# A decoder layer on one core: the first tile's two products by k tile, bias rows in eight transfers, memory preparation between down units

## The chip, the cores and the metric

The kernel runs on one core of a Trainium2 chip. The metric is device time in microseconds of one execution, the median of several runs. All data is float32. The matrix products are made in three passes of a reduced format (`fp32r`): each operand is split into a high and a low part, and hi x hi, lo x hi and hi x lo are summed.

## What is computed

One layer of a decoder, for 512 tokens of width 1024: a gated feed-forward block (FFN1), three mixers beside each other (sparse attention, a gated short convolution, attention into 256 memory tokens), and a second feed-forward block. The parts that matter here:

```python
def rmsnorm(x, g):
    y = xf * lax.rsqrt(jnp.mean(xf * xf, axis=-1, keepdims=True) + EPS)
    return y * g
def swiglu_ffn(h, w_in, w_out):                     # 1024 -> 2 x 2816 -> 1024
    a, b = jnp.split(h @ w_in, 2, axis=-1)
    return (jax.nn.silu(a) * b) @ w_out
x = x + 0.5 * swiglu_ffn(rmsnorm(x, ffn1_norm_g), ffn1_w_in, ffn1_w_out)
...
km, vm = jnp.split(rmsnorm(mem, mem_norm_g) @ w_mem_kv, 2, axis=-1)   # 256 memory tokens
...
bias = rel_bias[rel_bucket(dist)]                   # 16 heads, by distance; used in the attention
```

## The kernel before, in words

The tokens lie along the free axis: `xT` holds x as 8 k tiles of 128 x 512. `ffn(1, ...)` walks a fixed list of steps (`ffn_steps`). It has 22 feature tiles. Tiles 0 to 3 are made plainly (`up`): two products a and b, each of 8 k tiles by three passes, 24 matmuls of 512 columns (`mm3`, L419 to L421), into PSUM buffers `psg` and `pso`. Then a = silu(a) needs the row scale R. R comes from squares of x (`square_into`, ScalarE and VectorE), a sum over partitions on TensorE (L445), a Newton step on VectorE, four transposes on TensorE (L452) and a copy on ScalarE (L453). Tiles 4 to 21 are made from 2 x 2 blocks with seven products, P1 to P7 (`prod`, L545), 12 matmuls of 256 columns each, from other forms of the input (`Input.prep`) and of the weights (sums `sumS` on VectorE, L195). Between the products stand the `down` steps: eight per group of tiles, each multiplies a group's results by one column block of the second weight and adds it to `xT` on VectorE (L590, or `x1_done`, L665, in the last group). Each `down` needs one of two PSUM buffers `pss`.

Weights are loaded by SyncE's queue (SP, L183) in units of 128 x 1024 (512 KB) into four raw buffers, and split by `Weights._make`: ScalarE casts the high part `whi` (L227), VectorE subtracts to get the low part `wlo` (L228), six buffers of each. `ahead` makes the next part up to three uses early. A raw buffer that is free lets the next load go.

Work that has to be done at some time during FFN1 is a list of closures, `extra`: `more` runs the next one or two after a step. First the forms of the input (19 entries), then the bias table (4 entries: load, a product and its evacuation, a store of 16 rows to `scr`, and one transfer that repeats every row 128 times into `scr2`, L734), and, added when the products are done, the preparation of the memory tokens (10 entries: the load of `mT`, eight parts, a row scale), which so falls into the last eight `down` steps. A part is a scaled cast on ScalarE and the low half on VectorE (`mhi`, `mlo`, L457 and L458), and a square on ScalarE that VectorE adds up (L476, L477).

A scheduler then orders the instructions of each engine by dependences and program order; every engine runs its own list strictly in that order, and the two DMA queues (SP's and ScalarE's) issue in order too. The program's order sets what the scheduler prefers. The transfers of the two queues use the same 16 DMA engines. The start is written out by hand: one weight half, x tiles 0 to 2, the second half, x tiles 3 to 7.

Of the kernel before, what the change touches and what calls it, by code (L numbers as in the profile page):

```python
# [146 lines left out]
class Weights:  # L147
# [10 lines left out]
    def add(self, ap, key, width=512):  # L158
        j, n = len(self.units), ap.shape[1]
        self.units.append(ap)  # L160
        for c0 in range(0, n, width):
            c1 = min(c0 + width, n)
            self.specs.append((key, width, "raw", (j,), slice(c0, c1), (j,) if c1 == n else ()))

    def add_fast(self, a, b, f, name):

        if name == "P1":
            self.fast = getattr(self, "fast", {})
            self.fast[f] = (len(self.units), len(self.units) + 1)
            self.units += [a, b]  # L170
        j = self.fast[f]
        free = {"P2": j[:1], "P4": j[1:]}.get(name, ())
        self.specs.append((("prod", f, name), 512, FAST[name], j, None, free))


    def _dma(self, part=None):
        j = self.i_dma
        ap = self.units[j]
        n = ap.shape[1]
        if part != 1:  # L180
            self.raw[j] = self.pool.tile([128, 1024], F32, tag="wraw", name=f"wraw{j}", bufs=RAW_BUFS)
        c = slice(0, n) if part is None else slice(512 * part, 512 * part + 512)
        self.nc.sync.dma_start(self.raw[j][:, c], ap[:, c])  # L183
        if part != 0:
            self.i_dma += 1

    def prefetch(self):
        while self.i_free in self.freed:
# [67 lines left out]
class Input:  # L256
# [68 lines left out]
    def fast_done(self):  # L325
        self.stacks["late"].close()
        self.stacks["forms"].close()


class Layer:  # L330
# [29 lines left out]
    def unit_list(self):  # L360
        i = self.ins
        add = self.ws.add

        def ffn(n):
            w, wo = i[f"wf{n}i"], i[f"wf{n}o"]
            for step in ffn_steps(n):
                if step[0] == "up":
                    for ab in range(2):
                        add(w[step[1], ab], (n, "in", step[1], ab))
                elif step[0] == "down":  # L370
                    f0, f1 = FFN_GROUPS[step[1]]
                    add(wo[step[2]][:, f0 * 128:f1 * 128], (n, "out") + step[1:])
                else:
                    self.ws.add_fast(w[step[1], 0], w[step[1], 1], *step[1:])

        ffn(1)
        for c in range(4):
            for q in range(4):
                add(i["wmkv"][c, q], ("mkv", c, q))
        def tok(n, qs):  # L380
            for q in qs:
                add(i["t" + n][q][:, :TOK[n][0] * TOK[n][1][q]], ("tok", n, q), 304 if n == "s" else 512)

        def w1(kind, qs):
            for q in qs:
                add(i["w1" + "kv"[kind]][q], ("w1", kind, q))

        tok("c", range(4))
        tok("m0", [0, 1, 2])
        w1(0, [0])  # L390
        tok("m0", [3])
        w1(0, [1])
        tok("m1", [0])
        w1(0, [2])
        tok("m1", [1])
        w1(0, [3])
        tok("m1", [2])
        w1(1, [0])
        add(i["w2k"], ("w2", 0))
        w1(1, [1])  # L400
        tok("m1", [3])
        w1(1, [2, 3])
        tok("v", [0])
        add(i["w2v"], ("w2", 1))
        tok("v", [1, 2, 3])
        for n in ("s", "w", "q0", "q1"):
            tok(n, range(len(TOK[n][1])))
        for p in range(8):
            for t in range(6):
                add(i["wfeat"][p, t], ("feat", p, t))  # L410
        for m in range(NK):
            add(i["wout"][m], ("wout", m))
        ffn(2)


# [61 lines left out]
            nc.vector.tensor_tensor(acc, acc, sq[:, :src.shape[1]], op=ALU.add)  # L477


    def ffn(self, n, pool, x, done, before, extra, fast_done):  # L480

        nc, ws = self.nc, self.ws
        groups = FFN_GROUPS
        extra = list(extra)
        g, st = {}, {}

        def more(k=1):  # L490
            for fn in extra[:k]:
                fn()
            del extra[:k]

        def half_up(f, ab):
            whi, wlo = ws.use((n, "in", f, ab))
            p = self.ps("go"[ab])
            for k in range(NK):
                if k == NK // 2:
                    ws.ahead()  # L500
                    if f:
                        more()
                c = slice(k * 128, (k + 1) * 128)
                self.mm3(p, whi[:, c], wlo[:, c], x.hi[:, k], x.lo[:, k], k == 0, k == NK - 1)
            return p

        def act_a(p):
            a = pool.tile([128, 512], F32, tag="fa", name=self.nm("fa"), bufs=2)
            th = pool.tile([128, 512], F32, tag="fth", name=self.nm("fth"), bufs=2)
            nc.vector.tensor_tensor(a, p, x.R, op=ALU.mult)  # L510
            nc.scalar.activation(th, a, AF.Tanh, scale=0.5)
            nc.vector.scalar_tensor_tensor(a, th, 1.0, a, op0=ALU.add, op1=ALU.mult)
            nc.vector.tensor_tensor(a, a, x.R, op=ALU.mult)
            return a
# [3 lines left out]
            self.split(*g[f], a)  # L518

        def up(f):  # L520
            p = half_up(f, 0)
            if f > 0:
                a = act_a(p)
            if f:
                more()
            p2 = half_up(f, 1)
            if f == 0:
                before()
                a = act_a(p)
            nc.vector.tensor_tensor(a, a, p2, op=ALU.mult)  # L530
            put(f, a)
            if f:
                more()
# [45 lines left out]
        def down(gi, m):  # L579
            f0, f1 = groups[gi]  # L580
            nf = f1 - f0
            whi, wlo = ws.use((n, "out", gi, m))
            p = self.ps("s")
            for k in range(nf):
                if k == NK // 2:
                    ws.ahead()
                c = slice(k * 128, (k + 1) * 128)
                self.mm3(p, whi[:, c], wlo[:, c], g[f0 + k][0], g[f0 + k][1], k == 0, k == nf - 1)
            if gi < len(groups) - 1:
                nc.vector.scalar_tensor_tensor(self.xT[:, m], p, 0.25, self.xT[:, m], op0=ALU.mult, op1=ALU.add)  # L590
            else:
                done(m, p)
            more(2)

        steps = ffn_steps(n)
        for step, after in zip(steps, steps[1:] + [(None,)]):
            {"up": up, "prod": prod, "down": down}[step[0]](*step[1:])
            if step[0] == "up" and after[0] != "up":
                ws.sum_pool = x.plain_done()
                ws.ahead()  # L600
            elif step == ("prod", NF - 1, "P3"):
                ws.sum_pool = None
                x.fast_done()
                extra += fast_done()
        assert not extra

    def square_into(self, k, acc, src, sq):

# [7 lines left out]
    def run(self):  # L616
# [10 lines left out]
        self.scr2 = self.dram.tile([16, 128, WL], F32, name="scr2")  # L627

        nc.scalar.dma_start(self.small, ins["small"])
        self.ws._dma(part=0)  # L630
        for k in range(NK):
            nc.sync.dma_start(self.xT[:, k], ins["xT"][:, k])
            if k == 2:
                self.ws._dma(part=1)
        self.ws.prefetch()
        nc.vector.memset(self.ones, 1.0)

# [12 lines left out]

        x = Input(self, 1, fp, C_G1)
        for k in range(NK):
            x.put(k)
            if k in (0, 3):
                self.ws._make()

        def x_rstd():
            for k in range(NK):
# [14 lines left out]
        def fast_done():  # L673
            for h in (1, 0):
                mkp[h] = self.pool(memkv[h], f"mkp{h}", "right")
            made["pp"] = self.pool(prep, "pp", "right")
            return self.mem_prep(fp, made["pp"])

        self.ffn(1, fp, x, x1_done, x_rstd, x.prep() + self.bias_table(x), fast_done)
        pp = made["pp"]  # L680
        self.dump("x1", self.xT)

# [11 lines left out]
            self.split(self.Ahi[:, k], self.Alo[:, k], t)  # L694

        kfin = self.mem_kv(mkp, pp, [mix_rstd] + [lambda k=k: mix_h(k) for k in range(NK)])
        f1.close()


# [10 lines left out]
    def bias_table(self, x):  # L710
# [22 lines left out]
            src = self.scr[h:h + 1]  # L733
            nc.scalar.dma_start(self.scr2[h:h + n], bass.AP(src.tensor, src.offset, [[WL, n], [0, 128], [1, WL]]))  # L734

        return [load, table, store] + [lambda: repeat(0, 16)]

    def load_T(self, h):
        T = self.tp.tile([128, TW], F32, tag="T", name=f"T{h}", bufs=2)
# [2 lines left out]
        return T  # L742


    def mem_prep(self, fp, pp):
        self.mhi = pp.tile([128, NK, 256], F32R, name="mhi")
        self.mlo = pp.tile([128, NK, 256], F32R, name="mlo")
        mT = pp.tile([128, NK, 256], F32, tag="mT", name="mT")
        acc = pp.tile([128, 256], F32, name="macc")
        self.mrs = pp.tile([128, 2], F32, name="mrs")  # L750

        def part(k):
            self.prep_post(fp, k, mT[:, k], C_GMEM, self.mhi, self.mlo, acc)

        load = lambda: self.tc.keep_in_program_order(self.nc.scalar.dma_start(mT, self.ins["memT"]))
        return [load] + [lambda k=k: part(k) for k in range(NK)] + [lambda: self.token_rstd(pp, acc, 2, self.mrs)]

    def mem_kv(self, pools, pp, aux):

# [709 lines left out]
    def tail(self, mx1):  # L1469
# [27 lines left out]

        def fast_done():
            yp.append(self.pool(ys, "yp", "right"))
            return []  # L1500

        def y_done(m, p):
            y = yp[0].tile([128, 512], F32, tag="y", name=self.nm("y"), bufs=2)
            nc.vector.scalar_tensor_tensor(y, p, 0.25, self.xT[:, m], op0=ALU.mult, op1=ALU.add)
            nc.sync.dma_start(self.out[m], y)

        self.ffn(2, fp, x, y_done, x.rstd, x.prep(), fast_done)
        ys.close()
        f2.close()

# [81 lines left out]
```

## Time and profile before

| | us |
|---|---|
| median of 3 runs | 1412.68 |
| lowest, highest run | 1411.17, 1413.94 |
| the profiled execution, its whole time | 1415.84 |
| its span, first to last instruction | 1413.8 |
| TensorE (PE) busy | 1400.4 |
| VectorE (DVE) busy | 1094.1 |
| ScalarE (ACT) busy | 763.4 |

The profile lists every instruction of one execution with its start and duration, and for an engine's idle time the event that ended it. PE is the matmul unit, PEld its weight loads, which overlap. Matmul ends are modelled: a 512-column matmul is shown 0.39 us long though the next starts 0.23 us later, so TensorE's busy time hides small losses, and a wait of it begins up to 0.16 us before the idle time shown. PEclk is the granted TensorE clock, 1.00 for 2.4 GHz and 0.50 for 1.2 GHz. FFN1 ends at about 358 us.

### The profile page before, as it was taken

What the parts mean: (1) busy time and instruction counts of PE and PEld (TensorE: products, weight loads), DVE (VectorE), ACT (ScalarE), POOL (GpSimd) and SP (SyncE); (2) the same over time, 40 slices, a digit from 0 to 9 for tenths busy, and PEclk for the clock granted to TensorE, in tenths of its full rate; (3) what the DMA queues carried; (4) which work ended last, traced back from release to release, by engine and by line L of the source; (5) the groups of instructions that cost most, each with busy time, mean ns of one, the idle gap of its engine ahead of it and who ended that gap; (6) DMA issues with size and microseconds to landing.
All of it is one profiled execution on the core that took longest, in us unless ns stands there. A gap on an engine that the chain in (4) does not pass through costs nothing.

```text
span 1413.8 us, 22594 instructions
## 1 busy us (share of the span) xinstructions
PE 1400.4 (99%) x8211; PEld 1232.2 (87%) x8211; DVE 1094.1 (77%) x2496; ACT 763.4 (54%) x1723; POOL 1.3 (0%) x8
## 2 busy tenths in 40 slices
PE   8999999999999999999999999999999999999998
PEld 7889999998888889888888888888888899999997
DVE  7978877777876676778777887886767988787775
ACT  6445545445655755566666666666544555454542
POOL 0000000000000000000000000000000000000000
PEclk9999999999999999999999999999999999999999
DMA  5273233333552422232222222221232232323322
GB/s 188 70 273 112 91 104 107 104 96 121 165 165 89 146 76 82 84 97 67 77 68 85 73 68 75 68 90 61 61 104 77 74 126 90 120 90 102 104 93 99
DMA packets 49823, 142.86 MB, mean 101 GB/s; under 512 B 5472, under 2 KB 9856, under 8 KB 49584
## 3 DMA queue, kind: packets, MB, share of 16 engines
q1 hardware_dynamic: 47232, 134.83, 29.6%
q10 hardware_dynamic: 2480, 6.60, 1.4%
q8 instruction: 64, 1.05, 0.3%
q14 instruction: 47, 0.39, 0.1%
HBM read 139.27 MB, written 7.51 MB: 104 GB/s over the span
## 4 chain that ended last, share of the span: by engine, by line
PE 94%; DVE 3%; DMA 2%; ACT 1%; issue 1%; SPq 0%; ACTq 0%
PE pso L545 11%; PE psg L419 10%; PE psg L420 10%; PE psg L421 10%; PE pst L545 7%; PE psg L545 7%; PE pss L419 6%; PE pss L420 6%; PE pss L421 6%; PE pso L421 3%; PE pso L419 3%; PE pso L420 3%; PE pst L1309 3%; PE pso L1333 1%; PE pss L1267 1%; PE pss L1266 1%
## 5 line engine op out<-in xcount | busy, mean ns | idle before, releaser
L227 ACT CAST whi<-wraw 128x512 fp32r<-128x512 f32 (+2 forms) x458 | 275.4, 608 | 262.4 <-PE pss L420 59.5
L228 DVE TENSOR_TENSOR wlo<-wraw,whi 128x512 fp32r<-128x512 f32 (+2 forms) x458 | 305.2, 673 | 143.7 <-ACT whi L227 141.7
L419 PE MATMUL psg<-Ahi,whi 128*128 128x512 f32 x448 | 178.8, 399 | 0.0
L420 PE MATMUL psg<-Alo,whi 128*128 128x512 f32 x448 | 175.3, 391 | 0.0
L421 PE MATMUL psg<-Ahi,wlo 128*128 128x512 f32 x448 | 175.1, 391 | 0.0
L227 ACT CAST whi<-sumS 128x512 fp32r<-128x512 f32 x144 | 89.2, 621 | 125.8 <-PE pss L420 54.8
L419 PE MATMUL pss<-ghi,whi 128*128 128x512 f32 x352 | 138.4, 394 | 1.9 <-DVE xT L665 1.9
L420 PE MATMUL pss<-glo,whi 128*128 128x512 f32 x352 | 138.3, 393 | 0.0
L421 PE MATMUL pss<-ghi,wlo 128*128 128x512 f32 x352 | 137.5, 391 | 0.0
L1243 ACT ACTIVATE P<-P,nm 128x128 f32<-128x128 f32 (+3 forms) x128 | 72.2, 564 | 80.6 <-DVE nm L1242 79.6
L228 DVE TENSOR_TENSOR wlo<-sumS,whi 128x512 fp32r<-128x512 f32 x144 | 98.0, 683 | 6.7 <-ACT whi L227 6.6
L421 PEld LDWEIGHTS psg<-Ahi,wlo 128*128 128x128 f32 x448 | 84.1, 188 | 18.4
L419 PEld LDWEIGHTS psg<-Ahi,whi 128*128 128x128 f32 x448 | 84.3, 188 | 14.5 <-ACT Ahi L461 0.4
L420 PEld LDWEIGHTS psg<-Alo,whi 128*128 128x128 f32 x448 | 84.3, 188 | 14.0 <-DVE Alo L462 0.2
L545 PE MATMUL psg<-Ahi,whi 128*128 128x256 f32 x288 | 80.9, 281 | 0.0
L545 PE MATMUL psg<-Alo,whi 128*128 128x256 f32 x288 | 80.8, 281 | 0.0
L545 PE MATMUL psg<-Ahi,wlo 128*128 128x256 f32 x288 | 80.8, 281 | 0.0
L419 PEld LDWEIGHTS pss<-ghi,whi 128*128 128x128 f32 x352 | 66.5, 189 | 14.4 <-DVE xT L665 2.3
L421 PEld LDWEIGHTS pss<-ghi,wlo 128*128 128x128 f32 x352 | 66.5, 189 | 14.3
L590 DVE SCALAR_TENSOR_TENSOR xT<-pss,xT 128x512 f32<-128x512 f32 x80 | 54.9, 687 | 28.5 <-PE pss L421 28.3
L420 PEld LDWEIGHTS pss<-glo,whi 128*128 128x128 f32 x352 | 66.7, 190 | 11.5 <-DVE glo L462 0.2
L461 ACT CAST PThi<-pst 128x512 fp32r<-128x512 f32 (+3 forms) x128 | 54.3, 424 | 39.5 <-PE pst L1309 37.1
(368 smaller groups left out, 3667.6 us busy)
## 6 DMA issues: line engine op xcount, KB each, us to landing
wraw<-wfeat SPq DMA_DIRECT2D x48, 512.0 KB, 3.6
wraw<-wf2i SPq DMA_DIRECT2D x44, 512.0 KB, 3.2
wraw<-wf1i SPq DMA_DIRECT2D x43, 512.0 KB, 3.3
wraw<-wf1o SPq DMA_DIRECT2D x32, 256.0 KB, 3.2
wraw<-wmkv SPq DMA_DIRECT2D x16, 512.0 KB, 3.8
wraw<-wf2o SPq DMA_DIRECT2D x32, 256.0 KB, 3.2
scr<-scr ACTq DMA_DIRECT2D x1, 5248.0 KB, 27.0
T<-scr SPq DMA_DIRECT2D x16, 264.0 KB, 3.7
```

The costliest lines, as they stand in the source:

```text
L227: self.nc.scalar.copy(hi[:, :w], src)
L228: self.nc.vector.tensor_sub(lo[:, :w], src, hi[:, :w].bitcast(F32))
L419: mm(ps, ahi, bhi, start=start, stop=False)
L420: mm(ps, ahi, blo, start=False, stop=False)
L421: mm(ps, alo, bhi, start=False, stop=stop)
L461: self.nc.scalar.copy(hi, src)
L545: nc.tensor.matmul(p, a[:, c], b[:, k], start=k == 0 and i == 0 and name in ("P1", "P7"), stop=k == 3 and i == 2, skip_group_check=True)
L590: nc.vector.scalar_tensor_tensor(self.xT[:, m], p, 0.25, self.xT[:, m], op0=ALU.mult, op1=ALU.add)
L1243: self.nc.scalar.activation(P, P, AF.Exp, scale=-1.0, bias=nm, accum_out=ssum)
L1266: nc.tensor.matmul(p[:, :c1 - c0], hi[:, ts], K[:, c0:c1], start=True, stop=False)
L1267: nc.tensor.matmul(p[:, :c1 - c0], lo[:, ts], K[:, c0:c1], start=False, stop=True)
L1309: nc.tensor.transpose(p[:, (i - j) * 128:(i - j + 1) * 128], P[:, o:o + 128], self.ident)
```

## The change

Three things. First, for tile 0 of FFN1 the two products go k tile by k tile, six matmuls per k, over weight parts that hold 512 columns of both units; the first halves of both units are loaded ahead of x, the second halves after x tile 2. Second, the transfer that repeats the bias rows goes out in eight pieces of two rows. Third, the bias table and the memory preparation form a list of their own (`slow`), of which one entry runs after each `down` once `extra` is empty; the memory tiles move to another pool for that.

```diff
+    def add_pair(self, a, b, key):
+        j = len(self.units)
+        self.units += [a, b]
+        for h in range(2):
+            for i in range(2):
+                self.specs.append(((key, h), 512, "raw", (j + i,), slice(512 * h, 512 * h + 512), (j + i,) if h else ()))
+    def load_pair(self, h):
+        for j in range(2):
+            if h == 0:
+                self.raw[j] = self.pool.tile([128, 1024], F32, tag="wraw", name=f"wraw{j}", bufs=RAW_BUFS)
+            c = slice(512 * h, 512 * h + 512)
+            self.nc.sync.dma_start(self.raw[j][:, c], self.units[j][:, c])
+        self.i_dma = 2 * h
...
+        def first_up():
+            ps = [self.ps("go"[ab]) for ab in range(2)]
+            for h in range(2):
+                whi, wlo = ws.use(((n, "in", 0), h))
+                for k in range(4 * h, 4 * h + 4):
+                    if k % 4 == 2:
+                        ws.ahead()
+                    for ab in range(2):
+                        c = slice(512 * ab + k % 4 * 128, 512 * ab + k % 4 * 128 + 128)
+                        self.mm3(ps[ab], whi[:, c], wlo[:, c], x.hi[:, k], x.lo[:, k], k == 0, k == NK - 1)
+            return ps
...
         def up(f):
+            if f == 0 and n == 1:
+                p, p2 = first_up()
...
-            more(2)
+            if extra:
+                more(2)
+            elif slow:
+                slow.pop(0)()
...
-        self.ws._dma(part=0)
+        self.ws.load_pair(0)
         for k in range(NK):
             nc.sync.dma_start(self.xT[:, k], ins["xT"][:, k])
             if k == 2:
-                self.ws._dma(part=1)
+                self.ws.load_pair(1)
...
         for k in range(NK):
-            x.put(k)
             if k in (0, 3):
                 self.ws._make()
+                self.ws._make()
+            x.put(k)
...
-        self.ffn(1, fp, x, x1_done, x_rstd, x.prep() + self.bias_table(x), fast_done)
+        mem = ExitStack()
+        self.ffn(1, fp, x, x1_done, x_rstd, x.prep(), self.bias_table(x) + self.mem_prep(fp, mem), fast_done)
...
-        return [load, table, store] + [lambda: repeat(0, 16)]
+        return [load, table, store] + [lambda h=h: repeat(h, 2) for h in range(0, 16, 2)]
...
-    def mem_prep(self, fp, pp):
+    def mem_prep(self, fp, stack):
...
+        def load():
+            nonlocal mT, acc
+            mp = self.pool(stack, "mp", "left")
```

The scheduler moves instructions at three places. ScalarE at the start, before (`wraw_84` is the first weight unit, of its two halves; `xn` takes the squares):

```order
L227 CAST whi_146<-wraw_84 128x512
L457 ACTIVATE x1hi<-xT,small 128x512
L610 ACTIVATE xn_136<-xT 128x512
L457 ACTIVATE x1hi<-xT,small 128x512 x2
L612 ACTIVATE xn_136<-xT 128x512
L227 CAST whi_156<-wraw_84 128x512
```

and in the change (`wraw_84` and `wraw_86` are the two units; its lines are those of the new file):

```order
L240 CAST whi_145<-wraw_84 128x512
L240 CAST whi_149<-wraw_86 128x512
L472 ACTIVATE x1hi<-xT,small 128x512
L643 ACTIVATE xn_137<-xT 128x512
L472 ACTIVATE x1hi<-xT,small 128x512 x2
L645 ACTIVATE xn_137<-xT 128x512
L240 CAST whi_159<-wraw_84 128x512
L240 CAST whi_165<-wraw_86 128x512
L645 ACTIVATE xn_137<-xT 128x512
L472 ACTIVATE x1hi<-xT,small 128x512 x3
```

Two casts and one square stand between the third and the fourth `x1hi` now; before it was one square and one cast.

TensorE at tile 4, the first that is made with seven products, before (`pso_639` takes P6, `pst_684` the product of the bias table, `pst_640` P7):

```order
L421 MATMUL pss_665<-ghi_546,wlo_585 128x512
L545 MATMUL pso_639<-xP6hi_140,whi_634 128x256
...
L545 MATMUL psg_638<-Ahi,wlo_658 128x256
L419 MATMUL pss_758<-ghi_287,whi_688 128x512
L420 MATMUL pss_758<-glo_288,whi_688 128x512
L724 MATMUL pst_684<-oh,rb 128x512
L545 MATMUL pst_640<-xP7hi_142,whi_608 128x256
```

and in the change (`pst_641` takes P7, `pso_640` P6):

```order
L436 MATMUL pss_666<-ghi_553,wlo_586 128x512
L575 MATMUL pst_641<-xP7hi_143,whi_609 128x256
...
L575 MATMUL pst_641<-xP7hi_143,wlo_610 128x256
L575 MATMUL pso_640<-xP6hi_141,whi_635 128x256
...
L436 MATMUL pss_753<-ghi_553,wlo_686 128x512
L759 MATMUL pst_767<-oh,rb 128x512
```

All 12 matmuls of P7 moved from behind P6, P2 and the bias product to a place ahead of P6.

ScalarE in the middle of FFN1, in the change, at the load of the memory tile (before, `mT` is loaded and used in the last group of `down` steps):

```order
L791 DMA mT<-memT 128x2048
L582 ACTIVATE th_1986<-psg_1860 128x256
L240 CAST whi_2036<-sumS_35_1902 128x512
L240 CAST whi_2053<-wraw_1932 128x512
L240 CAST whi_2077<-sumS_39_2075 128x512
L472 ACTIVATE mhi<-mT,small 128x256
L488 ACTIVATE macc<-mT 128x256
...
L240 CAST whi_2123<-wraw_1930 128x512
L472 ACTIVATE mhi<-mT,small 128x256 x2
```

The parts of the memory tile now stand four instructions and more behind their load, in the middle of the block, several of them close together.

## Rows read from the trace of the kernel before

**Rows 1.** The page, busy time, share of the span and instructions of each engine.
```profile
PE 1400.4 (99%) x8211; PEld 1232.2 (87%) x8211; DVE 1094.1 (77%) x2496; ACT 763.4 (54%) x1723; POOL 1.3 (0%) x8
```

**Rows 2.** Waits of TensorE, whole span: for what, us in total, times, longest.
```profile
PE pso L545 <- DVE fth L571: 2.6, 1, 2.6
PE pss L419 <- DVE xT L665: 1.9, 1, 1.9
```

**Rows 3.** Windows: busy us and instructions per engine, PEclk, DMA share, GB/s.
```profile
27.30:68.00 40.70, 40.70 (x187) 33.73 (x185) 40.56 (x58) 19.07 (x28) 0.00 (x0) 1.00 0.19 59
...
84.00:110.00 26.00, 22.85 (x157) 21.50 (x157) 18.85 (x33) 11.71 (x25) 0.00 (x0) 0.93 0.74 261
...
132.00:330.00 198.00, 198.00 (x1383) 185.06 (x1382) 155.03 (x270) 95.81 (x192) 0.00 (x0) 1.00 0.32 101
...
9.40:15.00 5.60, 4.35 (x14) 2.46 (x15) 5.57 (x9) 5.60 (x11) 0.00 (x0) 1.00 1.03 415
...
105.30:108.70 3.40, 3.40 (x18) 3.40 (x17) 3.13 (x7) 0.90 (x2) 0.00 (x0) 0.50 0.66 237
...
351.10:354.40 3.30, 3.30 (x10) 2.52 (x9) 1.94 (x5) 1.54 (x4) 0.00 (x0) 0.50 0.00 0
```

**Rows 4.** Chain of waits that ended last, pieces: start, us, what.
```profile
2.11 6.55 DMA xT<-xT
...
110.38 1.36 PE pst L545 x12
...
130.78 0.23 PE pss L419
...
134.94 1.41 PE psg L545 x12
```

**Rows 5.** Timeline, first 22 us, ScalarE and TensorE: start, us, instruction, [idle before it].
```profile
8.68 0.72 ACT L457 ACTIVATE x1hi<-xT,small 128x512 fp32r<-128x512 f32 x1 [2.27 <-DMA xT<-xT]
...
9.83 0.60 ACT L227 CAST whi<-wraw 128x512 fp32r<-128x512 f32 x1
...
9.45 0.49 PE L419 MATMUL psg<-x1hi,whi 128*128 128x512 f32 x1 [1.47 <-ACT x1hi L457]
...
21.72 0.39 PE L419 MATMUL psg<-x1hi,whi 128*128 128x512 f32 x1
```

**Rows 6.** Timeline, 27 to 69 us, VectorE and TensorE.
```profile
27.32 0.69 DVE L510 TENSOR_TENSOR fa<-psg,Rx 128x512 f32<-128x512 f32 x1 [0.57 <-ACT Rx L453]
...
68.51 0.38 PE L545 MATMUL pso<-xP6hi,whi 128*128 128x256 f32 x1 [0.24 <-ACT whi L227]
```

**Rows 7.** DMA issues by tile: count, KB each, median us from issue to landing.
```profile
wraw<-wf1i SPq DMA_DIRECT2D x43, 512.0 KB, 3.3
...
scr<-scr ACTq DMA_DIRECT2D x1, 5248.0 KB, 27.0
...
scr<-bw ACTq DMA_DIRECT2D x1, 41.0 KB, 2.5
```

**Rows 8.** Tile `wraw`, issues from 83.8 to 90.4 us, four of them.
```profile
DMA to landing us min/median/max: 9.7/10.7/11.4
```

**Rows 9.** Timeline of TensorE, the stalls at 100 and 350 us.
```profile
100.38 0.38 PE L545 MATMUL pst<-xP7hi,wlo 128*128 128x256 f32 x1 [0.54 <-DVE wlo L228]
...
104.42 0.36 PE L545 MATMUL pso<-Ahi,whi 128*128 128x256 f32 x1 [2.62 <-DVE fth L571]
...
350.64 0.50 PE L419 MATMUL pss<-ghi,whi 128*128 128x512 f32 x1 [1.92 <-DVE xT L665]
```

**Rows 10.** Timeline, 149 to 158 us, VectorE and TensorE.
```profile
149.56 0.68 DVE L228 TENSOR_TENSOR wlo<-sumS,whi 128x512 fp32r<-128x512 f32 x1
...
157.15 0.28 PE L545 MATMUL pso<-xP6hi,whi 128*128 128x256 f32 x1
```

**Rows 11.** Waits, 105 to 338 us: for what, us in total, times, longest.
```profile
DVE sumS L195 <- DMA wraw<-wf1i: 8.7, 12, 1.2
```

**Rows 12.** Tile `mT`: operation, count, ns min/median/max, first and last start.
```profile
L458 DVE SCALAR_TENSOR_TENSOR mlo<-mT,small,mhi x8: 472/476/484, 346.1 to 352.6; 128x256 fp32r<-128x256 f32 x8
```

More of the change, by code (lines that the diff above doesn't have):

```diff
@@ L173, in add_fast, with _dma @@
         self.specs.append((("prod", f, name), 512, FAST[name], j, None, free))
-    def _dma(self, part=None):
+    def _dma(self):
         j = self.i_dma
[L178 to L185, printed above, removed]
+        n = self.units[j].shape[1]
+        self.raw[j] = self.pool.tile([128, 1024], F32, tag="wraw", name=f"wraw{j}", bufs=RAW_BUFS)
+        self.nc.sync.dma_start(self.raw[j][:, :n], self.units[j])
+        self.i_dma += 1
     def prefetch(self):
@@ L366, in ffn @@
             for step in ffn_steps(n):
-                if step[0] == "up":
+                if step == ("up", 0) and n == 1:
+                    self.ws.add_pair(w[0, 0], w[0, 1], (n, "in", 0))
+                elif step[0] == "up":
                     for ab in range(2):
@@ L477, in square_sum, with ffn @@
             nc.vector.tensor_tensor(acc, acc, sq[:, :src.shape[1]], op=ALU.add)
-    def ffn(self, n, pool, x, done, before, extra, fast_done):
+    def ffn(self, n, pool, x, done, before, extra, slow, fast_done):
         nc, ws = self.nc, self.ws
         groups = FFN_GROUPS
-        extra = list(extra)
+        extra, slow = list(extra), list(slow)
         g, st = {}, {}
@@ L520, in up @@
         def up(f):
[L521 to L526, printed above, removed]
+            if f == 0 and n == 1:
+                p, p2 = first_up()
+            else:
+                p = half_up(f, 0)
+                if f > 0:
+                    a = act_a(p)
+                    more()
+                p2 = half_up(f, 1)
             if f == 0:
@@ L603, in ffn @@
                 x.fast_done()
-                extra += fast_done()
-        assert not extra
+                fast_done()
+        assert not extra and not slow
     def square_into(self, k, acc, src, sq):
@@ L676, in fast_done @@
             made["pp"] = self.pool(prep, "pp", "right")
-            return self.mem_prep(fp, made["pp"])
-        self.ffn(1, fp, x, x1_done, x_rstd, x.prep() + self.bias_table(x), fast_done)
+        mem = ExitStack()
+        self.ffn(1, fp, x, x1_done, x_rstd, x.prep(), self.bias_table(x) + self.mem_prep(fp, mem), fast_done)
         pp = made["pp"]
@@ L696, in run @@
         kfin = self.mem_kv(mkp, pp, [mix_rstd] + [lambda k=k: mix_h(k) for k in range(NK)])
+        mem.close()
         f1.close()
@@ L742, in load_T @@
         return T
-    def mem_prep(self, fp, pp):
[L746 to L750, printed above, removed]
+    def mem_prep(self, fp, stack):
+        mT = acc = None
+        def load():
+            nonlocal mT, acc
+            mp = self.pool(stack, "mp", "left")
+            self.mhi = mp.tile([128, NK, 256], F32R, name="mhi")
+            self.mlo = mp.tile([128, NK, 256], F32R, name="mlo")
+            mT = mp.tile([128, NK, 256], F32, name="mT")
+            acc = mp.tile([128, 256], F32, name="macc")
+            self.mrs = mp.tile([128, 2], F32, name="mrs")
+            self.tc.keep_in_program_order(self.nc.scalar.dma_start(mT, self.ins["memT"]))
         def part(k):
             self.prep_post(fp, k, mT[:, k], C_GMEM, self.mhi, self.mlo, acc)
-        load = lambda: self.tc.keep_in_program_order(self.nc.scalar.dma_start(mT, self.ins["memT"]))
-        return [load] + [lambda k=k: part(k) for k in range(NK)] + [lambda: self.token_rstd(pp, acc, 2, self.mrs)]
+        return [load] + [lambda k=k: part(k) for k in range(NK)] + [lambda: self.token_rstd(fp, acc, 2, self.mrs)]
     def mem_kv(self, pools, pp, aux):
@@ L1499, in fast_done @@
             yp.append(self.pool(ys, "yp", "right"))
-            return []
         def y_done(m, p):
@@ L1505, in y_done @@
             nc.sync.dma_start(self.out[m], y)
-        self.ffn(2, fp, x, y_done, x.rstd, x.prep(), fast_done)
+        self.ffn(2, fp, x, y_done, x.rstd, x.prep(), [], fast_done)
         ys.close()
```

## The prediction

> **What bounds the kernel now.** I read the page first: TensorE is busy for 1400.4 of 1413.8 us [rows 1], so nothing but its lost time can be won, some 13 us of idle at most and whatever it loses at half clock. Then the waits of TensorE, sorted: the two longest are 2.6 us on VectorE's `fth` and 1.9 us on VectorE's `xT` [rows 2]. Then the windows, to see what stands around each wait [rows 3]: from 84 to 110 us TensorE is busy for 22.85 of 26 us at a mean clock of 0.93 while the DMA engines are 74% busy; in 105.3 to 108.7 and in 351.1 to 354.4 the granted clock is 0.50, that is 1.2 instead of 2.4 GHz, each time right after one of the two longest waits. The reader should see there that three places in the first feed-forward block (FFN1) hold nearly all that this change can reach: the start, the stall at 100 us and the one at 349 us. The order of instructions after FFN1 is the same on TensorE in both kernels, so I give it nothing.
>
> **The start (first tile by k).** Before, the two products of the first tile need 48 matmuls, one per 0.23 us when nothing waits [rows 4], 11.0 us; the next tile begins at 21.72 [rows 5]. At 9.45 six of them are done and TensorE has sat idle for 1.47 us, so 42 x 0.23 = 9.7 us would end at 19.1. Everything that could be won is 21.72 - 19.1 + 1.5 = 4.1 us.
>
> The limit is ScalarE, which makes `x1hi` from tiles of x that land late: the third was issued at 2.11 and took 6.55 us [rows 4], so the cast began at 8.68 [rows 5]. It was the fourth transfer of the queue. From then on the engines move 415 GB/s [rows 3], 0.63 us per 256 KB. In the changed queue two weight halves stand ahead of x instead of one, so I take x1 for the fourth (8.7), x2 at 9.3, the second weight halves until 10.6 and x3 at 11.2. ScalarE's order then reads x1, x2, square, two casts, square, x3 to x5, square, x6, x7. With 0.72 us for an `x1hi` and 0.60 for a cast [rows 5], overlapping a little, and 0.6 for a square (the rest between those rows), x2 is done at 10.1, the casts at 11.9, x3 at 13.2, x7 at 16.4; VectorE's low halves come some 0.7 us later. TensorE does six matmuls per k, 1.38 us: k1 from 9.4 to 10.9, k2 to 12.3, a wait of 0.9, k3 from 13.2 to 14.7, then four more groups, to 20.2. That is about 1.4 us earlier than 21.72.
>
> Does it last? From 27.3 to 68 us VectorE is busy for 40.56 of 40.7 us [rows 3], starting with the first operation that needs the row scale R at 27.32 [rows 6]; there it, not TensorE, sets the pace, and at 68.51 TensorE waits 0.24 us on the cast behind it. R does not come sooner (its squares still end on ScalarE at about 22). By widths VectorE has as much work between R and that point as before, 39.6 against 39.5 us at 0.60 per 512 columns. But the order piece on TensorE shows P7's 12 matmuls (1.4 us) moved ahead of P6, the step that waits: TensorE reaches P7 1.4 us earlier, fills the time until P6's weights are there, and has P7 behind it. So I let the start keep **1.3 us** of its 1.4; the ends are a gain of 4.1 and a loss of 1.3 (two transfers' delay reaching the tile whole).
>
> **The eight transfers.** One issue of 5,248 KB took 27.0 us, against 3.3 for a weight tile [rows 7]; the four weight tiles issued meanwhile took 9.7 to 11.4 us [rows 8], late by 6.4 to 8.1. VectorE's sums wait for them, and TensorE behind VectorE: idle 0.54 at 100.38 and 2.62 at 104.42 [rows 9]. Each idle figure starts at the modelled end of a matmul (0.28 us long, one per 0.12), so 0.16 more is lost each time: 3.5 us. Then 3.4 us at half clock, half of it lost, about 1.6. Against that, TensorE ran 12 small matmuls in 1.36 us after the stall, until 130.8, and in 1.41 from 133 on [rows 4]; without the stall I expect the slower pace, 16 blocks x 0.05 = 0.8. Net 3.5 + 1.6 - 0.8 = **4.3 us** back.
>
> A piece has 1/8 of the bytes, 27.0 / 8 = 3.4 us of the engines, and the order shows one about every half tile of FFN1. If a weight tile has one whole piece ahead, it lands 3.4 us later. What hides this is the lead of the weight parts: the low half for P6 begins at 149.56 and lasts 0.7, its matmuls begin at 157.15 [rows 10], a lead of 7 us. VectorE has no such lead on the DMA, it already waits 8.7 us in 12 waits [rows 11], but in 132 to 330 it is busy for 155 of 198 us [rows 3], so 3.3 us of a 15.2 us tile (13 tiles in that stretch) are free. Seven more issues on ScalarE cost nothing: it is busy for 96 of 198 us there [rows 3].
>
> The Trainium skill speaks against this part (DMA: Bandwidth & Descriptors, Rules for kernel authors and Anatomy of one DMA): few transfers of a MiB or more, because each carries a fixed 2.0 us on top of its bytes at 436 GB/s. By that formula, given for another queue, one transfer takes an estimated 14.3 us and eight take 28.6, so by it the split costs 14 us of the engines that the one transfer didn't. The trace's 27.0 us for one [rows 7] does not agree with the first figure, and no run yet shows the second; what a fixed part per piece would do here is the slower rival below.
>
> **The memory parts.** They leave the last group of FFN1. Before, their 16 VectorE operations (eight of about 0.48 us [rows 12]; eight squares and sums beside them) stood ahead of `xT`, whose PSUM buffer TensorE needed: idle 1.92 us at 350.64 [rows 9], plus 0.16 for the overlap, then 3.3 us at half clock [rows 3], 1.6 lost. Together **3.7 us**, all of it gone, since what stays there is 512, 512 and 384 columns of VectorE per product, 1.65 us at 0.60 per 512, beside nine matmuls, 2.07 us. Where they go to, the order piece on ScalarE shows: not one by one behind the products, but close together behind the load, in some 38 instructions of VectorE's order. That adds about 6 us of VectorE to a stretch of two tiles, where 6.6 are free and 7 us of lead hide the rest: nothing on TensorE.
>
> **Sum.** -1.3 - 4.3 - 3.7, and +0.5 for waits in the middle that I cannot place: -8.8 us. The profiled execution took 1415.84 us, so it becomes 1407.0; the median of the runs is 3.2 us lower, 1412.68, and becomes **1403.9**. A measurement tells about 0.2% (2.8 us) from no change.
>
> **Rivals.**
> - *The start gives nothing* (14%). VectorE is full from 27.3 to 68 [rows 3]; if P7's own weights are late too, TensorE just waits longer at 68. With two gaps near 1 us in the first tile growing past the 1.47 us that left the clock at full [rows 3, 5], half clock would cost 1.6 more. For it: two more transfers ahead of x. Against it: P7's place. 1403.9 + 1.3 + up to 1.6: 1405 to 1407.
> - *The pieces and memory parts push VectorE into the middle* (13%). If every piece delays the second tile of a pair by the whole 3.4 us, two per tile for four tiles give 27 us on VectorE; four tiles absorb 13 and the lead 7, TensorE gets up to 7. Half of that is likelier: about 1407 to 1409.
> - *Slower* (6%). A piece costs more than its share of the bytes: a transfer of only 41 KB took 2.5 us [rows 7], so a piece may hold a weight tile by 3.4 + 2.5 = 5.9 us. Two per tile for four tiles are 47 us on VectorE; 13 are free and 7 us of lead cover, so TensorE could lose 27, and it decides from a third of that, 9.3 us. Waits of about 2 us, as at 350.64, would bring half clock, 1.6 us each, besides. About 1415 to 1420. Against it: most of a landing time is latency that runs beside other transfers, as the weight tiles' 3.3 us for 1.3 us of bytes at 415 GB/s. This is what the fixed part in the Trainium skill's DMA page would come to if none of it overlapped.
> - *More from the start* (6%). If x1 lands at its old time and R moves too, up to 2.8 us more: 1401.
> - *It does not do what it says* (3%): a transfer in pieces that still fills the engines as one, because all pieces are issued while the first is under way. ScalarE's order puts 8 to 13 instructions between them, so I hold it for unlikely; 1408 then.
>
> **How the numbers follow.** The forecast has 58%, from 1402 to 1405.5. The range takes in the start's rivals on both sides and most of the second: 1400.5 to 1409.0; outside are the slower case and the ends of the others. Faster by over 0.2%, under 1409.9: the forecast, the start's two cases (14 and 6%) and 12 of the other 16%, 0.90. Within 0.2%: the remaining 4%. Slower: 0.06.
>
> **What would show it.** Right: no wait of TensorE over 1 us between 10 and 360 us, and no stretch of FFN1 at clock 0.50; the second tile's first matmul at 20 to 20.6; weight tiles of 75 to 150 us landing in under 7 us; no idle before the first `xT` of the last group; twelve small matmuls in 1.41 us from 84 to 130. Wrong: VectorE's sums waiting more than 15 us in total for `wf1i`; a stretch at half clock near 15, 68 or 150 to 200 us; TensorE's idle at 68 grown past 1 us. It would be wrong as a whole if the time after 360 us changed by more than 1 us.

## The result and the profile after

The changed kernel takes 1451.20 us, the median of 4 runs (1450.28 to 1451.53); the kernel before, run beside it, 1413.31 us (1411.17 to 1416.15). The ratio is 1.0266, 95% interval 1.0246 to 1.0285. The forecast was 1403.9 us, in a range of 1400.5 to 1409.0: wrong, and on the wrong side.

| | before | after |
|---|---|---|
| span of the profiled execution | 1413.8 us | 1449.7 us |
| first matmul of the second tile | 21.72 us | 19.73 us |
| first matmul on the memory tiles, behind FFN1 | 365.08 us | 400.93 us |
| from there to the end of the span | 1048.7 us | 1048.8 us |

The profiled execution of before, at 1415.84 us, is one of the longer ones: of 53 runs of this kernel beside the experiments, the 29 with a mean granted clock of 0.999 or more have a median of 1412.2 us, the 16 at 0.997 or less one of 1414.6.

The loss lies wholly in FFN1: 400.93 - 365.08 = 35.9 us, and the spans differ by 35.9. The page of after, sections 1 and 2, against [rows 1]; in section 2 each column is a fortieth of the span, 36 us:

```profile
PE 1409.9 (97%) x8211; PEld 1240.4 (86%) x8211; DVE 1092.3 (75%) x2496; ACT 760.0 (52%) x1723; POOL 1.3 (0%) x8
...
PE   9996689999999999999999999999999999999998
...
PEclk9998889999999999999999999999999999999999
DMA  5242233323453351222222221212122232332332
```

The dip is in columns 4 to 6, 108 to 217 us. In before the stall of 100 us was one, of some microseconds [rows 2]; now TensorE waits again and again. Its waits in 75 to 240 us (for what, us in total, times, longest), and the window of the same stretch (busy us and instructions per engine, PEclk, DMA share, GB/s):

```profile
PE pso L575 <- ACT u L593: 13.4, 3, 5.8
PE pso L575 <- DVE fth L601: 6.6, 2, 5.8
PE pso L575 <- ACT pso L587: 5.8, 1, 5.8
PE pso L575 <- ACT whi L240: 3.3, 1, 3.3
```

```profile
75.00:240.00 165.00, 132.60 (x876) 123.01 (x875) 100.44 (x184) 62.23 (x137) 0.00 (x0) 0.90 0.34 112
```

TensorE is idle for 165 - 132.60 = 32.4 us. Most of it ends with ScalarE, but ScalarE is busy for only 62 of 165 us, and the DMA engines are used to 34%. Neither looks like a bound. The next view does: ScalarE's timeline (start, us, instruction, idle before it), where `ACTq` rows are what its sequencer does.

```profile
109.20 10.75 ACTq L769 DMA_DIRECT2D scr<-scr  x1
...
119.99 0.36 ACT L587 COPY pso<-psg 128x256 f32<-128x256 f32 x1 [9.14 <-issue]
...
120.38 14.20 ACTq L769 DMA_DIRECT2D scr<-scr  x1
...
134.62 0.62 ACT L476 CAST ghi<-fa 128x512 fp32r<-128x512 f32 x1 [11.64 <-issue]
```

The *issue* of one bias transfer holds ScalarE's sequencer for 10.75 and 14.20 us; the engine finishes what it had been given before and then stands for 9.14 and 11.64. It runs its instructions in order, so PSUM evictions and casts wait behind the issue, and TensorE behind them: its wait that ends at 120.40 is 5.76 us. All eight issues in one line (min/median/max of one in ns, first and last start in us):

```profile
L769 ACTq DMA_DIRECT2D scr<-scr x8: 593/11400/14195, 78.5 to 165.9; - x8
```

Together they take 67.6 us. The one issue of before, for eight times the bytes, took 0.62 us. Why a small transfer should take longer to issue than a large one is in the DMA view, queue by queue (packets, MB, share of 16 engines; `q10` is ScalarE's queue, and a packet of it is a row of the bias table). First after, 130 to 136 us, where no weight is under way; then before, 79 to 83 us:

```profile
q10 hardware_dynamic: 115, 0.30, 12.9%
```

```profile
q10 hardware_dynamic: 537, 1.41, 103.2%
```

12.9% of sixteen engines is about two of them: 0.30 MB in 6 us, 50 GB/s. The one transfer of before kept all sixteen busy, 1.41 MB in 4 us. So a piece is an eighth of the bytes on an eighth of the engines. A row of 2,624 bytes takes an engine 0.129 x 16 x 6 us / 115 = 0.108 us, and a piece of 256 rows on two engines 13.8 us.

### The profile page after: what moved, and what is told of

Read it like the earlier page. It is cut to its first block, busy times and chain, and to the rows that moved or that the text cites. A ratio compares the mean times of both kernels' runs of the same rounds, so it can differ in the third digit from the quotient of the medians.

```text
span 1449.7 us, 22575 instructions
## 1 busy us (share of the span) xinstructions
PE 1409.9 (97%) x8211; PEld 1240.4 (86%) x8211; DVE 1092.3 (75%) x2496; ACT 760.0 (52%) x1723; POOL 1.3 (0%) x8
## 4 chain that ended last, share of the span: by engine, by line
PE 89%; DMA 4%; DVE 4%; issue 2%; ACT 1%; SPq 0%; ACTq 0%; DVEq 0%
PE psg L434 10%; PE psg L435 10%; PE psg L436 10%; PE pso L575 10%; PE pst L575 6%; PE psg L575 6%; PE pss L434 6%; PE pss L435 6%; PE pss L436 6%; DMA scr<-scr 3%; PE pso L436 3%; PE pso L434 3%; PE pso L435 3%; PE pst L1349 2%; PE pso L1373 1%
## 5 line engine op out<-in xcount | busy, mean ns | idle before, releaser
L435 PEld LDWEIGHTS psg<-Alo,whi 128*128 128x128 f32 x448 | 84.3, 188 | 14.1 <-DVE Alo L477 0.2
L434 PEld LDWEIGHTS pss<-ghi,whi 128*128 128x128 f32 x352 | 66.6, 189 | 12.3 <-ACT ghi L476 0.2
```

The costliest lines, as they stand in the source:

```text
L434: mm(ps, ahi, bhi, start=start, stop=False)
L435: mm(ps, ahi, blo, start=False, stop=False)
```

## The experiments

Times of before are those of runs on the same chip: 1413.39, 1412.83 and 1412.95 us for the first four, the next four and the last three.

**1. One copy in the changed kernel.** Only the last line of the bias list goes back:

```diff
-[lambda h=h: repeat(h, 2) for h in range(0, 16, 2)]
+[lambda: repeat(0, 16)]
```

> The changed kernel with the bias rows in one 16-row copy again; the pair at the start and the moved memory parts stay. Theory A (the eight two-row copies move only two packets at a time, fill ScalarE's DMA queue, and ScalarE stands in the issue of the next copy): the whole loss goes, ScalarE's issues take under 1 us each, and what is left is the start (-1.7 us by the changed trace) and the memory tail (-3.7): 1408 us (1405 to 1411), with the pause and half clock near 105 us back. Theory B (the memory parts, one by one in the down units, hold VectorE and so the weights): over 1435 us. Theory C (the paired first tile starts a shift that the later tiles pay for): over 1435 us.

Measured: 1413.57 us (12 runs, 1411.87 to 1414.86), ratio 1.0001 (0.9993 to 1.001). The loss is gone, so theories B and C fall. But the time lies above A's range too: the 5 us of the start and the memory parts do not show. TensorE's timeline tells where the start went:

```profile
88.92 0.38 PE L575 MATMUL pso<-xP6hi,wlo 128*128 128x256 f32 x1 [1.15 <-DVE wlo L241]
...
102.13 0.48 PE L575 MATMUL pst<-xP7hi,whi 128*128 128x256 f32 x1 [3.50 <-ACT whi L240]
106.56 0.36 PE L575 MATMUL pso<-Ahi,whi 128*128 128x256 f32 x1 [1.09 <-DVE fth L601]
```

These are 5.74 us of idle against 3.16 in before [rows 9]. The copy now lands at 105.56 instead of 104.14 us, so the matmuls that come 2.3 us earlier up to there (the 350th, counted from 0, at 76.22 instead of 78.48) only wait longer: the 600th is at 118.02 instead of 116.79. The memory parts did pay: between the 800th matmul and the first on the memory tiles lie 218.8 us instead of 222.6. (At these places both kernels have run the same matmuls; elsewhere their orders differ.) The spans say 2.0 us faster, the medians see nothing: the execution of before that was profiled is 2.5 us longer than its median here.

**2. The eight copies in the kernel before.** The same line, the other way round, in before.

> The kernel before with only the copy split in eight two-row copies. A: slower by about as much as the whole change, 1445 to 1470 us, with ScalarE's issues of the copies together over 55 us long and two packets of the copies in flight at a time; as the other list issues them closer together, the queue fills by the third or fourth copy. B and C: 1409 us, the gain that was forecast for this part, or at most no change (1413).

Measured: 1490.77 us, ratio 1.0549 (1.0531 to 1.0568): A, but 21 us above its range, since this order puts the eight issues one behind the other. ScalarE's timeline has them as one row, and TensorE one wait:

```profile
76.53 84.66 ACTq L734 DMA_DIRECT2D scr<-scr  x8
161.29 0.62 ACT L227 CAST whi<-wraw 128x512 fp32r<-128x512 f32 x1 [84.16 <-DMA scr<-scr]
```

```profile
PE pss L419 <- ACT whi L227: 75.5, 1, 75.5
```

The `DMA scr<-scr` in the second row is the transfer whose issues held ScalarE.

**3. The eight copies with their repeats outermost.** The same bytes in the same eight pieces; only the order of the dimensions in the descriptor changes:

```diff
-nc.scalar.dma_start(self.scr2[h:h + n], bass.AP(src.tensor, src.offset, [[WL, n], [0, 128], [1, WL]]))
+nc.scalar.dma_start(self.scr2[h:h + n].rearrange("n p w -> p n w"),
+                    bass.AP(src.tensor, src.offset, [[0, 128], [WL, n], [1, WL]]))
```

> The changed kernel with the same eight copies of two rows, but each written with its 128 repeats as the outermost dimension. A, if it is how a copy is cut into parallel pieces that matters: about 16 packets at a time, each 656 KB copy done in 2 to 4 us, issues under 1 us, no wait of TensorE in FFN1 after 30 us, and with it all three forecast gains: 1403.5 us (1402 to 1407). Rival D (eight copies are bad for their number, by the semaphores that weight loads share with them or by issue time): over 1425 us. If the outermost dimension does not matter: 1451 as the change.

Measured: 1406.35 us, ratio 0.9949 (0.9936 to 0.9962): 44.9 us below the change, by this alone. Issues and queue, 77 to 110 us:

```profile
L769 ACTq DMA_DIRECT2D scr<-scr x8: 537/538/641, 77.5 to 102.9; - x8
```

```profile
q10 hardware_dynamic: 2186, 5.38, 50.0%
```

No issue is over 0.64 us; all rows pass in these 33 us, where the change needed 132 (from 78 to 210). A copy lands after 5.5 to 9.8 us, not the 2 to 4 expected. D falls: it is not the number of transfers. TensorE keeps two kinds of waits in 75 to 400 us, 0.7 us in all, against 32.4 in the change.

**4. Spacing them: a run that missed.** To see whether the full queue or the two held engines costs the time, an empty entry was put behind each two-row copy.

> The changed kernel with an empty part behind each two-row copy, so one is issued every second down unit (about 15.3 us apart) instead of every one (7.6). A copy alone takes 256 packets x 0.110 us / 2 = 14 us, so the queue never holds two full copies. A (the full queue stops ScalarE): issues under 1 us, and the loss nearly gone: 1403 to 1412 us. Rival E (the copies hold two of the sixteen DMA engines against the weight loads for 8 x 14 = 112 us, whether or not ScalarE stands): over 1430 us, weight tiles landing after 6 us and more.

Measured: 1452.18 us, ratio 1.0268. That decides nothing. The copies are not among the instructions that the program holds in order, and their places on ScalarE came out as in the change: the issues begin at 78.2, 87.1, 98.3 and 111.3 us (78.6, 88.3, 99.4 and 109.2 in the change) and take up to 14.1 us. The list is not the order.

**5. Spacing them, held in place.** As 4, with each copy wrapped in `keep_in_program_order(...)`.

> The spacing that the run before missed: every copy held at its place in program order, with an empty part behind it, so that the eight two-row copies stand one in every second down unit (about 15.3 us). A (a full queue stops ScalarE in the issue): 256 rows x 0.110 us / 2 = 14 us fits the gap, issues under 1 us, ScalarE never stands in an issue, and nearly all of the loss goes: 1403 to 1413 us. Rival E (two DMA engines held against the weight loads, 112 us in all, are enough): 1425 us or more with issues short.

Measured: 1418.81 us, ratio 1.0046 (1.0028 to 1.0064). Of the 44.9 us, 32.4 are gone, but 12.5 stay, above A's range and below E's. The trace divides them cleanly. The window of 75 to 240 us, and the DMA issues of 121 to 222 us (count, KB each, median us to landing):

```profile
75.00:240.00 165.00, 163.94 (x1188) 154.85 (x1188) 132.09 (x231) 78.15 (x164) 0.00 (x0) 1.00 0.39 132
```

```profile
wraw<-wf1i SPq DMA_DIRECT2D x12, 512.0 KB, 6.2
scr<-scr ACTq DMA_DIRECT2D x7, 656.0 KB
wraw<-wf1o SPq DMA_DIRECT2D x12, 256.0 KB, 7.3
```

The weight tiles land after 6.2 and 7.3 us instead of 3.3 [rows 7] and 3.2, for a hundred microseconds, and TensorE does not care: its clock is 1.00, and the 1.06 us that are missing belong to one wait that ends at 240.36, by the cause below. SP's queue waits 12.0 us for copies there and harms nobody. So E falls: two engines held do not hurt by themselves. What is left is one place behind that window:

```profile
232.15 5.23 ACTq L791 DMA_DIRECT2D mT<-memT  x1
...
251.28 0.51 ACT L472 ACTIVATE mhi<-mT,small 128x256 fp32r<-128x256 f32 x1 [11.61 <-DMA mT<-memT]
```

```profile
253.84 0.58 PE L575 MATMUL pso<-xP6hi,whi 128*128 128x256 f32 x1 [9.11 <-ACT pso L587]
```

The memory tiles' load stands on the same queue behind the last copies: its issue takes 5.23 us and it lands 19.1 us after it began, against 0.36 and 5.5 in experiment 3. ScalarE, in order, stands 4.42 us behind the issue and then 11.61 before its first operation on the tiles, and TensorE 9.11 behind it, then at clock 0.50. The first of these is A again. The second is neither A nor E: ScalarE waits for data that came through the same queue behind copies on two engines.

**6. Four copies of four rows.** `repeat(h, 4)`, `range(0, 16, 4)`.

> The changed kernel with four copies of four rows. If rows of the outermost dimension set how many packets move at once, four do: each copy still takes 128 x 0.110 = 14 us, but there are four of them, and the queue (which held about 445 rows at two packets at a time, 222 for each) is filled at most just at the third or fourth. A: ScalarE stands under 5 us in issues, 1404 to 1414 us. E (held engines against weight loads): half the copy time of the change on twice the engines, about half the loss, 1425 us or more.

Measured: 1418.87 us, ratio 1.0041 (1.0025 to 1.0057), above A's range and below E's. My arithmetic for the queue was wrong, as ScalarE stands:

```profile
98.30 4.63 ACTq L769 DMA_DIRECT2D scr<-scr  x1
...
109.91 10.03 ACTq L769 DMA_DIRECT2D scr<-scr  x1
```

16.5 us of issues give 12.5 us of loss against experiment 3. Over the kernels the loss grows with that time: 67.6 us of issues and 44.9 lost, 84.7 and 79.1 (experiment 2 against 8). What is outstanding when an issue ends can be counted. At the ends of the change's fourth to seventh issues, q10 had moved 585, 841, 1097 and 1353 rows since the first; 1024, 1280, 1536 and 1792 were issued: 439 each time. At the end of the eighth it is 2048 - 1560 = 488. With four rows at the last two ends it is 1536 - 660 = 876 and 2048 - 1188 = 860. So an issue of these copies ends when some 215 to 245 rows for each engine are outstanding. For the memory tiles' load it was another number: its issue in experiment 5 ended with 2048 - 1901 = 147 rows left on the two engines. What sets the number stays open. One copy of 16 rows puts 128 on each, and passes; a two-row copy also puts 128 on each of its two, and the third finds them full. The first window of these:

```profile
q10 hardware_dynamic: 585, 1.52, 9.7%
```

**7. Without the pair**, from experiment 3's kernel, the first tile's products one after the other as in before:

```diff
-if step == ("up", 0) and n == 1:
-    self.ws.add_pair(w[0, 0], w[0, 1], (n, "in", 0))
-elif step[0] == "up":
+if step[0] == "up":
...
-self.ws.load_pair(0)
+self.ws._dma(part=0)
```

> The kernel with eight copies at sixteen packets and the moved memory parts, but the first tile's two products one after the other again, as in the kernel before. The pair gave 3.2 us at the end of the first tiles in that kernel's trace (matmul 330 at 72.04 us against 75.25): if it lasts, 1409.5 us here against 1406.35 with the pair (ratio 1.002). If VectorE, full to 68 us, would have eaten it, 1406 as with the pair.

Measured: 1406.47 us, ratio 0.9956 (0.994 to 0.9971), the same as with it. The pair's lead over this kernel was 1.07 us at the 330th matmul (72.04 against 73.11) and 0.05 at the 800th (136.85 against 136.90). So most of the 3.2 us that the expectation gave to the pair are not its own. This kernel, too, has P7 ahead of P6, which the list `slow` brought and not the pair, and at the 330th before has already run the two matmuls of the bias product, which come later here. At the 350th, where all have run the same ones, it is 78.48 in before, 77.10 here and 76.04 with the pair.

**8. The kernel before with eight copies at sixteen packets**, issued one behind the other.

> The kernel before with its copy as eight copies at sixteen packets; here the order puts all eight issues one behind the other, so the rows come as densely as in the one copy. Theory F (what helps is that the copies are spread over the weight loads): no change, 1412 to 1414.5 us, pause near 104 us back. Theory G (many small copies leave the weight loads more room than one large one, spread or not): 1409 to 1411 us.

Measured: 1411.67 us, ratio 0.9992 (0.9983 to 1.0002): between F and G, not told from no change. In its trace the longest wait of 75 to 240 us is 1.5 us instead of 2.6, and no half clock follows it. By the medians, cutting alone does little; what the trace says of it stands under *What the term was worth*.

**9. The copies of experiment 3 held in place, one per down unit**, with the pair, without it, and with sixteen one-row copies.

> Eight copies at sixteen packets, each held at its place in program order, one per down unit, the pair and the moved memory parts kept. Theory H (the pair's 2.1 us were given back in the 0.75 us of waits for weights between 105 and 130 us and in a slower pace behind them, all made by the copies still bunched in 77 to 109 us): with the copies spread the waits go and the pair shows: 1404.5 to 1405.8 us. Theory I (VectorE and the weight stream behind it set the pace to 135 us whatever the start): 1406 to 1407 us.

> The same without the pair at the start. H: 1406 to 1407, one to two us above the run with the pair. I: equal to it within 0.5 us.

> As wide_kept with sixteen one-row copies, one per down unit, so each weight load meets half the rows. H: within 0.5 us of wide_kept, as that has no wait left to remove; if copies of 656 KB still hold weights up, 0.5 to 1 us faster. The memory parts start eight down units later and should cost nothing, as each copy is done in 2 to 4 us.

Measured: 1405.48 us, ratio 0.9961 (0.9944 to 0.9978); 1407.90 (1406.18 to 1416.30), 0.9978 (0.9962 to 0.9994), above H's 1406 to 1407; 1405.20, 0.995 (0.9937 to 0.9963). The first has no wait of TensorE in 30 to 400 us, and in it and the last the window of 75 to 240 us is full; the first:

```profile
75.00:240.00 165.00, 165.00 (x1200) 156.19 (x1199) 139.15 (x251) 88.42 (x185) 0.00 (x0) 1.00 0.44 144
```

The pair is 1.38 us ahead at the 330th matmul (72.12 against 73.50) and still 1.38 at the 800th (135.78 against 137.16), the spans differ by 1.5: that the lead lasts, as H says, holds in the traces. Its size is that of one pair of executions: the one without the pair ran at clock 0.50 from 10.8 to 14.2 us, and its second tile begins 0.40 later than in experiment 7. The medians agree in sign, but their intervals overlap. Sixteen copies bring nothing over eight that can be told. Theirs is the lowest median of all, under that of the kernel before by about 7.7 us, and under that of the change by 46.

## Why the prediction was wrong, step by step

**The eight transfers: the step that failed.** "A piece has 1/8 of the bytes, 27.0 / 8 = 3.4 us of the engines." The rate of the one transfer was taken over to a piece, and with it that "seven more issues on ScalarE cost nothing". A piece takes 13.8 us, on two engines, and the issues 67.6 us of ScalarE. The -4.3 of this term is, with all else kept, 1451.20 against 1413.57 of experiment 1: +37.6. No row of before showed a copy with an outermost dimension of two. Its upper bound, 5.9 us for a piece, added a small transfer's latency to a share of the bytes, and nowhere asked how many engines would carry it. The clue stood in the diff: the piece's outermost dimension falls from 16 to 2.

The shapes decide it; experiment 3 changes the order of the dimensions alone. Outermost 2, 4, 16 and 128 kept about 2 (12.9% of sixteen), 4 (23.5% in 112 to 120 us of experiment 6), 16 (103%) and again many (50% beside the weights) engines busy. The line of experiment 6:

```profile
q10 hardware_dynamic: 277, 0.72, 23.5%
```

The Trainium skill says so in the page that the prediction cites for another rule (DMA: Bandwidth & Descriptors, Why a DMA increments its semaphore by 16 and not by 1): a transfer runs on the largest number of engines up to 16 that divides the slowest dimension of size over one on both sides. The first three of these traces agree with it in number; that of 128 is shown only to use many. By it a piece is two engines' work, which with the 0.108 us per row above is 13.8 us. The rule of the Trainium skill's page that I weighed instead, a fixed 2 us on each transfer, does not decide this case: experiment 3 has eight transfers too and is 7.0 us faster than before, and experiment 8, in the kernel before, is not slower. (By that rule eight such transfers take an estimated 28.3 us, not the prediction's 28.6; nothing hangs on it.)

The *slower* rival had the right sign at 6%, and neither its mechanism (a weight tile held up by a piece) nor its size (1415 to 1420): weight tiles that land after 6 to 7 us cost nothing in experiment 5. The rival that the pieces "still fill the engines as one" was the reverse of what came.

**What the term was worth.** From the 350th to the 800th matmul, between which these three kernels run the same ones, before takes 63.99 us, experiment 8 60.47 and the last kernel without the pair 59.67. So in the traces cutting at full width gave 3.5 us and the pieces apart 4.3, as forecast. The medians show less of it: 1.2 us for experiment 8, not told from no change. The mechanism was right, and the size in the traces, for pieces on many engines and apart.

**The start.** 1.4 us earlier at the second tile was forecast, 20.2; it begins at 18.59 to 19.73 in the eight traces with the pair, and at 20.74 to 21.72 in the five without, so sooner than thought. That 1.3 us of it last is right in number, and partly by luck. In experiment 9 the pair leads by 2.64 us at the second tile (18.83 against 21.47), by 2.33 at the first matmul of P7 (65.54 against 67.87) and by 1.37 at the 350th (76.12 against 77.49). So about 1 us goes at P6, near 68 us, where the rival *the start gives nothing* had looked for it. It goes in pieces too short to be shown as idle time: P6's first matmul comes 0.42 us after P7's last, with the pair, and 0.11 without. The gain was larger than forecast and so was the loss. And P7's place, which was to keep the gain, is the same without the pair. Wherever copies bunch behind it, in 88 to 130 us, the rest of the lead goes too: in experiment 7's comparison it falls from 1.07 to 0.05 us by the 800th.

**The memory parts.** -3.7 forecast. Between the 1,500th matmul and the first on the memory tiles, the change takes 119.00 us (400.93 - 281.93), before 122.83 (365.08 - 242.25): -3.8. No wait and no stretch at clock 0.50 is left there. Right.

**The signs to watch.** Wrong, as the prediction said what would show it: a stretch at half clock in 150 to 200 us, and VectorE's sums waiting 21.3 us for `wf1i`, in 75 to 240 us:

```profile
DVE sumS L208 <- DMA wraw<-wf1i: 21.3, 6, 7.6
```

After 360 us nothing changed by more than the 0.1 us above: right. With the copies at full width and apart the time comes near the forecast: 1403.9 was forecast, 1405.5 is what experiment 9 gives with pair and eight copies. The spans differ by 10.5 us there (1413.8 - 1403.3), the medians by 7.5, against 8.8 forecast. The prediction priced its terms in one trace, and that execution is 2.9 us longer than the median of the runs beside experiment 9; it took the whole gain off the median all the same.

## What to carry to other kernels

When a transfer is cut up, look at the outermost dimension of each piece on both sides: here it, not the bytes, set how many engines carried it; 16 and 128 kept many busy, 2 and 4 did not. An issue on a compute engine's queue is free only while the rows fit behind it, so put the duration of the issue rows beside the engine's idle time: "issue" as a releaser of ScalarE means that ScalarE itself stands. A gain ahead of a stall that another engine times is not a gain until that stall is gone. And before a gain is read off one trace, compare that execution's time with the median.

## What was not expected of the hardware

An issue of these copies holds its engine until all but some 215 to 245 rows for each DMA engine are done, so the first three of eight copies took 1.2, 0.6 and 4.1 us to issue, and the next five 10.8 to 14.2. Nothing marks this as a wait: the engine's row is a DMA instruction, and its followers show "issue" (in experiment 2 the transfer's name). And with each of TensorE's six long waits, of 2.67 to 5.83 us, came a stretch at half clock, as with the two of before [rows 3]; its waits of 1.15 and 1.53 us had none. The window behind the wait of 5.76 us:

```profile
120.40:125.00 4.60, 4.60 (x21) 4.60 (x22) 3.82 (x7) 2.58 (x6) 0.00 (x0) 0.50 0.42 149
```

TensorE's idle time in 75 to 240 us is 32.4 us, and the mean clock there 0.90. The six stretches at 0.50 last 34.1 us, and TensorE is busy for 24.56 of them; half of that, an estimated 12.3 us, is lost. With the 31.7 us by which the idle time exceeds that of experiment 3 this makes 44.0 of the 44.9 us.
